# Tables of the rotary angles held behind the last row tile of h instead of the first one

## The chip, the cores and the metric

The kernel runs on one core of a Trainium2 chip. The metric is the device time in microseconds (us) of one execution. Engines are named as in the profile: PE is TensorE's matmul, PEld its weight load, DVE is VectorE, ACT is ScalarE, POOL is GpSimd, SP is SyncE, whose queue issues most transfers. Each engine works through its own instructions in order; waits between engines go by semaphores.

## The reference, cut to what matters

One decoder layer: `h = layer_norm(x) * (1 + scale1) + shift1` with modulation vectors from `silu(c) @ w_ada`, then one input projection of h, from which a causal convolution branch (c_val, c_gate) and a retention branch (q, k, v, g) go on, then an output projection and a gated MLP. What the change touches is the rotation of q and k:

```python
half = x.shape[-1] // 2
inv_freq = ROPE_BASE ** (-jnp.arange(half, dtype=jnp.float32) / half)
ang = positions.astype(jnp.float32)[..., None] * inv_freq
cos = jnp.cos(ang)[:, :, None, :]
sin = jnp.sin(ang)[:, :, None, :]
x1, x2 = x[..., :half], x[..., half:]
return jnp.concatenate([x1 * cos - x2 * sin, x2 * cos + x1 * sin], axis=-1)
```

There are 512 tokens, D_MODEL = 1024, 8 heads of width 128 for q and k.

## The kernel before, in words

All matrix products run as three fp32r products of high and low halves, so a weight and an activation are each split by a copy (the high half, on ACT) and a subtraction (the low half, on DVE).

The first stage, lines 463 to 488, runs over k = 0 to 7, the eight row tiles of h (128 channels by 512 tokens each). In each round `mod_pair` takes two dot products of 1024 on DVE (L378) for the scale and the shift of tile k, PE transposes the normalised x into `xT` (L453), ACT makes `hf` from it (L454) and its high half (L456), DVE the low half (L457), and PE multiplies with six units of weights `w0h`, `w0l` (L480, L481, L484), 18 matmuls of 512 columns. The six sums `u0` to `u5` stay in six of the eight PSUM banks: c_val, c_gate, q, k and two of g for head 0. The other two banks take the transposes.

Behind that stage come the values of heads 0 and 1 (`values`, L554 to L556): 96 matmuls into four banks `v`, with four pieces of weights (`wh`, `wl` 0 to 3 here, made at L146 and L147; three buffers of each). Two of the banks `v` are those of the transposes. The other two come free when ACT has read c_gate (`th`, L515, a tanh) and c_val (`cv`, L517), the first steps of `conv`. `rotary` then reads q and k with the tables `ctab` and `stab` (L534, L535).

`rotary_tables` (L408 to L438) makes these two tables from the positions: the angle in two halves `A1`, `A2`, then five rounds that reduce it modulo a turn, each a pair on ACT that rounds into `tr` (L419, L420) and a step on DVE that takes the fraction `fr` (L424), which is added into `sm` (L428). One more rounding of `fr` stands in the fifth round (L427). Then, for each table, one rounding of `sm`, L433, L434 and four Sin on ACT (L438). `tr`, `fr` and `sm` have one buffer each, so that a round waits for the one before.

The order of instructions on an engine is set when the kernel is built, by a scheduler that takes what is ready by priority. `later(150)` gives the tables a priority 150 steps back, so that they fill gaps. `tc.issue_after(done.ins)` holds all of them until the instruction named has been placed: `done` is the last low half of h (L457) of the round. The 30 taps of a convolution (L525) have the lowest priority (`later(500)`) and fill DVE up through the heads.

Of the kernel before, what the change touches and what calls it, by code (L numbers as in the profile page):

```python
# [20 lines left out]
ND = D // P  # L21
# [157 lines left out]
def block_kernel(ctx: ExitStack, tc: tile.TileContext, a, out):  # L179
# [7 lines left out]
    @contextmanager  # L187
    def later(n):
        p = tc.cur_priority
        tc.cur_priority = p + n  # L190
        yield
        tc.cur_priority = p
# [23 lines left out]
    def vc(name, j=0, w=1):  # L216
        o, _ = VEC[name]
        return vec[:, o + j:o + j + w]
# [38 lines left out]
    def split_to(h, l, src, scale=None):  # L257
        act(h, src, AF.Copy)
        tt(l, src, h.bitcast(F32), ALU.subtract)
# [64 lines left out]
    def ft(tag, shape, dt=F32, bufs=1):  # L324
        uid[0] += 1
        return fp.tile(list(shape), dt, tag=tag, bufs=bufs, name=f"{tag}_{uid[0]}")
# [28 lines left out]
    def load_first(k):  # L355
        wa = ft("wa", [P, 2048], bufs=3)
        w = ft("w0", [P, 768], bufs=3)
        if k == 1:
            nc.sync.dma_start(w, a["w0"][k])
            nc.sync.dma_start(wa, a["wada"][k])  # L360
        else:
            nc.sync.dma_start(wa[:, :D], a["wada"][k][:, :D])
            nc.sync.dma_start(wa[:, D:], a["wada"][k][:, D:])
            nc.sync.dma_start(w, a["w0"][k])
        return wa, w
# [24 lines left out]
    def norm_x(s):  # L390
        rs, nb = layer_stats(xh[s])
        for j in range(2):
            act(xh[s][j], xh[s][j], AF.Identity, bias=nb, scale=rs)
# [14 lines left out]
    def rotary_tables():  # L408
        nc.vector.tensor_copy(A, posi)
        ts(A, A, cc("freq"), None, ALU.mult)  # L410
        nc.vector.tensor_copy(A1r, A)
        tt(A2, A, A1, ALU.subtract)
        c1, c2, c3, c4, c5 = C2PI
        ts(sm, A1, c5, None, ALU.mult)
        for src, c in ((A2, c4), (A1, c4), (A2, c3)):
            stt(sm, src, c, sm, ALU.mult, ALU.add)

        def rnd(dst, src, c=1.0):
            act(dst, src, AF.Identity, bias=cc("magic"), scale=c)  # L419
            act(dst, dst, AF.Identity, bias=cc("magic", 1))  # L420

        for src, c in ((A2, c2), (A1, c3), (A2, c1), (A1, c2), (A1, c1)):
            rnd(tr, src, c)
            stt(fr, src, c, tr, ALU.mult, ALU.subtract)  # L424
            if src is A1 and c == c1:
                rnd(tr, fr)
                tt(fr, fr, tr, ALU.subtract)  # L427
            tt(sm, sm, fr, ALU.add)  # L428
        for tab, shift in ((stab, 0.0), (ctab, 0.25)):
            if shift:  # L430
                ts(sm, sm, shift, None, ALU.add)
            rnd(tr, sm)
            tt(sm, sm, tr, ALU.subtract)  # L433
            ts(fr, sm, 0.49999994, -0.49999994, ALU.min, ALU.max)  # L434
            for half in range(2):
                for dst in range(2):
                    sgn = -1.0 if (dst == 0 and not shift) else 1.0
                    act(tab[64 * dst:64 * dst + 64, half * NT:(half + 1) * NT],  # L438
                        fr[64 * half:64 * half + 64], AF.Sin, scale=sgn * TWO_PI)

    def mod_pair(j, src):
        for t in range(2):
            dot(mods[:, 2 * j + t:2 * j + t + 1], src[:, t * D:(t + 1) * D])
        tt(mods[:, 2 * j:2 * j + 2], mods[:, 2 * j:2 * j + 2], bada[:, 2 * j:2 * j + 2], ALU.add)
# [4 lines left out]
    def first_h(k, hf, c):  # L449

        pt = ps("xT")
        for s in range(c.start // P, c.stop // P):
            nc.tensor.transpose(pt[:, s * P:(s + 1) * P], xh[s][k // 4][:, (k % 4) * P:(k % 4 + 1) * P], ident)  # L453
        act(hf[:, c], pt[:, c], AF.Identity, bias=mods[:, 2 * k + 1:2 * k + 2], scale=mods[:, 2 * k:2 * k + 1])  # L454
        hh, hl = h_h[:, k, c], h_l[:, k, c]
        (act(hh, hf[:, c], AF.Copy) if k else nc.vector.tensor_copy(hh, hf[:, c]))  # L456
        return tt(hl, hf[:, c], hh.bitcast(F32), ALU.subtract)  # L457

    for k in range(ND):
        if k + 2 < ND:  # L460
            lf.append(load_first(k + 2))
        if k == ND - 2:
            st.load(0)
        if k == ND - 1:
            st.load(1)
        wa, w0 = lf[k]
        mod_pair(k, wa)
        hf = ft("hf", [P, S], bufs=2)
        wh = base.tile([P, 768], F32R, tag="wh", bufs=3, name=f"w0h{k}")
        wl = base.tile([P, 768], F32R, tag="wl", bufs=3, name=f"w0l{k}")  # L470
        for n, c in enumerate((slice(0, 256), slice(256, 512)) if k == 0 else (slice(0, 512),)):
            if n:
                norm_x(2)
                norm_x(3)
            done = first_h(k, hf, c)
            if not n:
                split_to(wh, wl, w0)
            for u in range(6):
                w = slice(u * P, (u + 1) * P)
                mm(acc0[u][:, c], wh[:, w], h_h[:, k, c], start=(k == 0 and n == 0), stop=False, skip_group_check=True)  # L480
                mm(acc0[u][:, c], wh[:, w], h_l[:, k, c], start=False, stop=False, skip_group_check=True)  # L481
            for u in range(6):
                w = slice(u * P, (u + 1) * P)
                mm(acc0[u][:, c], wl[:, w], h_h[:, k, c], start=False, stop=(k == ND - 1), skip_group_check=True)  # L484
        if k == 0:
            with later(150), tc.issue_after(done.ins):
                rotary_tables()
            nc.gpsimd.tensor_scalar(bhalf, vc("bin", E_CV, 32), 0.5, None, ALU.mult)
# [39 lines left out]
    def rotary(i, pq, e, nm):  # L528
        sw = ht("sw", [P, S])
        b = vc("bin", e)  # L530
        act(sw[0:64], pq[64:128], AF.Identity, bias=b[64:128])
        act(sw[64:128], pq[0:64], AF.Identity, bias=b[0:64])
        f = ht("t1", [P, S], bufs=2)
        stt(f, pq, b, ctab, ALU.add, ALU.mult)  # L534
        tt(sw, sw, stab, ALU.mult)  # L535
        tt(f, f, sw, ALU.add)
        xh_ = ht(nm + "h", [P, S], F32R, bufs=2 if nm == "q" else 1)
        xl_ = ht(nm + "l", [P, S], F32R, bufs=2 if nm == "q" else 1)
        split_to(xh_, xl_, f)
        return f, xh_, xl_  # L540
# [150 lines left out]
    for i in range(NH):  # L691
        if i == 0:
# [3 lines left out]
            k = rotary(i, pk, E_K + i, "k")  # L696
            v2 = values(i)
        else:
# [14 lines left out]
            k = rotary(i, pk, E_K + i, "k")  # L713
# [149 lines left out]
    for j in range(ND):  # L863
        p_ = ps("yb")
        for half in range(2):
            wh, wl = st.get()
            for kk in range(8):
                k = 8 * half + kk
# [320 lines left out]
    for n, R in enumerate((R1, R2, R2, R2, R1, R3)):  # L1189
# [3 lines left out]
        for q in range(6):  # L1193
# [16 lines left out]
            for kk in range(2 if q < 5 else 1):  # L1210
                k = 2 * q + kk
# [147 lines left out]
```

## Time and profile before

| | |
|---|---|
| median of 3 runs | 1053.08 us (1052.61 to 1053.3) |
| the profiled execution | 1051.99 us |
| its span in the trace | 1050.2 us |
| PE busy | 1025.7 us (98%) |
| DVE busy | 837.3 us (80%) |
| ACT busy | 494.5 us (47%) |

The span is the part of the execution that the trace covers; 1.8 us lie around it. Times in rows are us from the start of the span. A row of the order of time has the start, the busy time, the engine, the line, the operation, output and inputs, and in brackets the idle time of the engine before it with what ended that. In the table of stretches each engine has its busy time and its number of instructions.

### The profile page before, as it was taken

The numbers are of one execution on the slowest core, as the hardware profiler recorded it, in microseconds if no ns is written. First come the engines' busy times: TensorE is split into PE (matmuls) and PEld (weight loads), VectorE is DVE, ScalarE is ACT, GpSimd is POOL, SyncE is SP. The second block draws the span as 40 slices with busy tenths as digits, with TensorE's granted clock in tenths as the row PEclk, the third lists the DMA queues.
The fourth block names the chain that finished last, engine by engine and source line by source line (L and its number), as shares of the span: only waits on it lengthen the run. The fifth ranks groups of instructions, "written<-read, shape, count | busy, mean of one in ns | idle before, by whom it ended". The sixth has DMA issues, their size and how long they took to land.

```text
span 1050.2 us, 12939 instructions
## 1 busy us (share of the span) xinstructions
PE 1025.7 (98%) x4889; PEld 858.6 (82%) x4889; DVE 837.3 (80%) x1373; ACT 494.5 (47%) x766; POOL 72.2 (7%) x93
## 2 busy tenths in 40 slices
PE   5999999999999999999999999999999999999996
PEld 4778888888888888888888888899888888888785
DVE  7979999999789979789994445876666666669888
ACT  5675444443454354461353334264444444457661
POOL 1000302020211020000000000110000000000012
PEclk9999999999999999999999999999999999999998
DMA  9733745482749286368653246012223223245772
GB/s 343 280 107 137 193 146 124 165 190 88 190 154 198 93 252 153 120 227 296 235 224 120 81 165 255 21 41 89 113 81 108 94 87 115 81 155 186 252 218 91
DMA packets 57009, 164.50 MB, mean 157 GB/s; under 512 B 4337, under 2 KB 27121, under 8 KB 47218
## 3 DMA queue, kind: packets, MB, share of 16 engines
q1 hardware_dynamic: 43328, 139.11, 37.9%
q0 software_dynamic: 13328, 24.38, 10.9%
q8 instruction: 38, 0.62, 0.2%
q10 hardware_dynamic: 290, 0.18, 0.1%
q14 instruction: 25, 0.20, 0.1%
HBM read 161.56 MB, written 25.17 MB: 178 GB/s over the span
## 4 chain that ended last, share of the span: by engine, by line
PE 89%; DVE 4%; ACT 3%; DMA 2%; issue 1%; POOL 0%; SPq 0%; DVEq 0%; ACTq 0%; POOLq 0%
PE up L506 7%; PE up L507 7%; PE up L509 7%; PE yb L870 3%; PE gate L506 3%; PE gate L507 3%; PE yb L871 3%; PE yb L872 3%; PE gate L509 3%; PE v L554 3%; PE v L556 3%; PE v L555 3%; PE g L507 2%; PE g L506 2%; PE g L509 2%; PE o L644 2%
## 5 line engine op out<-in xcount | busy, mean ns | idle before, releaser
L147 DVE TENSOR_TENSOR wl<-stage,wh 128x1024 fp32r<-128x1024 f32 x177 | 212.5, 1202 | 100.9 <-PE up L509 57.4
L146 ACT ACTIVATE wh<-stage 128x1024 fp32r<-128x1024 f32 x177 | 184.7, 1044 | 219.5 <-PE up L507 56.1
L525 DVE SCALAR_TENSOR_TENSOR conv<-ci,vec,conv 128x512 f32<-128x512 f32 x240 | 176.8, 747 | 3.4
L506 PE MATMUL up<-h,wh 128*128 128x512 f32 x304 | 118.3, 389 | 0.0
L507 PE MATMUL up<-h,wh 128*128 128x512 f32 x304 | 118.3, 389 | 0.0
L509 PE MATMUL up<-h,wl 128*128 128x512 f32 x304 | 75.1, 389 | 0.0
L509 PEld LDWEIGHTS up<-h,wl 128*128 128x128 f32 x304 | 57.1, 188 | 11.9
L506 PEld LDWEIGHTS up<-h,wh 128*128 128x128 f32 x304 | 57.1, 188 | 11.8
L507 PEld LDWEIGHTS up<-h,wh 128*128 128x128 f32 x304 | 57.1, 188 | 11.8
L1169 PE MATMUL d<-wh,op 128*128 128x512 f32 x132 | 51.4, 391 | 0.7 <-DVE dtmp L1226 0.6
L1170 PE MATMUL d<-wh,op 128*128 128x512 f32 x132 | 51.4, 389 | 0.0
L1171 PE MATMUL d<-wl,op 128*128 128x512 f32 x132 | 51.2, 389 | 0.0
L554 PE MATMUL v<-wh,h 128*128 128x512 f32 x128 | 49.9, 390 | 0.9 <-ACT th L515 0.9
L870 PE MATMUL yb<-rh,wh 128*128 128x512 f32 x128 | 50.3, 393 | 0.0
L506 PE MATMUL gate<-h,wh 128*128 128x512 f32 x128 | 50.1, 392 | 0.0
L872 PE MATMUL yb<-rh,wl 128*128 128x512 f32 x128 | 49.9, 389 | 0.0
L507 PE MATMUL gate<-h,wh 128*128 128x512 f32 x128 | 49.8, 389 | 0.0
L555 PE MATMUL v<-wh,h 128*128 128x512 f32 x128 | 49.8, 389 | 0.0
L871 PE MATMUL yb<-rl,wh 128*128 128x512 f32 x128 | 49.8, 389 | 0.0
L556 PE MATMUL v<-wl,h 128*128 128x512 f32 x128 | 49.8, 389 | 0.0
L1060 ACT ACTIVATE u<-up,vec 128x512 f32<-128x512 f32 x44 | 34.3, 779 | 25.1 <-PE up L509 21.7
L507 PE MATMUL g<-h,wh 128*128 128x512 f32 x112 | 43.7, 390 | 0.0
(317 smaller groups left out, 2398.9 us busy)
## 6 DMA issues: line engine op xcount, KB each, us to landing
stage<-in_wup SPq DMA_DIRECT2D x22, 1024.0 KB, 4.8
stage<-in_wstep SPq DMA_DIRECT2D x21, 1024.0 KB, 4.8
wb<-in_wada SPq DMA_DIRECT2D x32, 512.0 KB, 5.6
stage<-in_wstep SPq DMA_DIRECT2D x16, 512.0 KB, 9.4
stage<-in_wret SPq DMA_DIRECT2D x8, 1024.0 KB, 5.2
stage<-in_wga SPq DMA_DIRECT2D x8, 1024.0 KB, 4.8
wa<-in_wada SPq DMA_DIRECT2D x14, 512.0 KB, 7.1
stage<-T SPq DMA_DIRECT2D x6, 1024.0 KB, 4.8
```

Source lines behind the costliest of these rows:

```text
L146: nc.scalar.activation(wh[:, :w], src, AF.Copy)
L147: nc.vector.tensor_tensor(wl[:, :w], src, wh[:, :w].bitcast(F32), ALU.subtract)
L506: mm(dst, wh[:, k * P:(k + 1) * P], hs[k][0], start=(k == 0), stop=False)
L507: mm(dst, wh[:, k * P:(k + 1) * P], hs[k][1], start=False, stop=False)
L509: mm(dst, wl[:, k * P:(k + 1) * P], hs[k][0], start=False, stop=(k == n - 1))
L525: stt(o, ci[:, t:t + S], vc("cw", i * CK + t), o, ALU.mult, ALU.add)
L554: mm(pv[s], h_h[:, k, sl], wh[:, r], start=(k == 0), stop=False)
L555: mm(pv[s], h_l[:, k, sl], wh[:, r], start=False, stop=False)
L556: mm(pv[s], h_h[:, k, sl], wl[:, r], start=False, stop=(k == ND - 1))
L870: mm(p_, wh[:, w], rs_[k][0], start=(k == 0), stop=False)
L871: mm(p_, wh[:, w], rs_[k][1], start=False, stop=False)
L872: mm(p_, wl[:, w], rs_[k][0], start=False, stop=(k == 15))
```

## The change

`rotary_tables()` with its hold and the small `bhalf` step after it is called in the last round of the row tiles (k = 7) and no longer in the first (k = 0). `done` is then the low half of the last row tile. The instructions are the same.

```diff
@@ -482,7 +482,7 @@
             for u in range(6):
                 w = slice(u * P, (u + 1) * P)
                 mm(acc0[u][:, c], wl[:, w], h_h[:, k, c], start=False, stop=(k == ND - 1), skip_group_check=True)
-        if k == 0:
+        if k == ND - 1:
             with later(150), tc.issue_after(done.ins):
                 rotary_tables()
             nc.gpsimd.tensor_scalar(bhalf, vc("bin", E_CV, 32), 0.5, None, ALU.mult)
```

On DVE at the end of the row tiles, before; `h_163` is the low half of h, `w0l` and `wl` are low halves of weights, `tr`, `fr`, `sm` and `A` belong to the tables:

```order
L444 TENSOR_TENSOR mods<-mods,bada 128x2
L457 TENSOR_TENSOR h_163<-hf_521,h_162 128x512
L424 SCALAR_TENSOR_TENSOR fr_161<-A_23_157,tr_160 128x256
L259 TENSOR_TENSOR w0l_562<-w_68_473,w0h_561 128x768
L457 TENSOR_TENSOR h_163<-hf_560,h_162 128x512
L427 TENSOR_TENSOR fr_161<-fr_161,tr_160 128x256
L428 TENSOR_TENSOR sm_159<-sm_159,fr_161 128x256
L147 TENSOR_TENSOR wl_663<-stage_513,wh_662 128x1024
L147 TENSOR_TENSOR wl_667<-stage_513,wh_666 128x1024
L433 TENSOR_TENSOR sm_159<-sm_159,tr_160 128x256
```

The same place with the change:

```order
L444 TENSOR_TENSOR mods<-mods,bada 128x2
L457 TENSOR_TENSOR h_163<-hf_472,h_162 128x512
L457 TENSOR_TENSOR h_163<-hf_511,h_162 128x512
L409 CAST A_156<-pos_118 128x256
L259 TENSOR_TENSOR w0l_513<-w_68_424,w0h_512 128x768
L410 TENSOR_SCALAR A_156<-A_156,cst 128x256
L411 CAST A_23_157<-A_156 128x256
L147 TENSOR_TENSOR wl_663<-stage_464,wh_662 128x1024
L412 TENSOR_TENSOR A_24_158<-A_156,A_23_157 128x256
L147 TENSOR_TENSOR wl_667<-stage_464,wh_666 128x1024
L414 TENSOR_SCALAR sm_159<-A_23_157 128x256
L424 SCALAR_TENSOR_TENSOR fr_161<-A_24_158,tr_160 128x256
```

Before, the tables are in their fifth round here; with the change their first step stands here.

On ACT at the seventh and eighth row tile (k = 6 and 7), before:

```order
L454 ACTIVATE hf_521<-xT_524,mods 128x512
L419 ACTIVATE tr_160<-A_23_157,cst 128x256
L456 ACTIVATE h_162<-hf_521 128x512
L420 ACTIVATE tr_160<-tr_160,cst 128x256
L454 ACTIVATE hf_560<-xT_563,mods 128x512
```

With the change:

```order
L454 ACTIVATE hf_472<-xT_475,mods 128x512
L454 ACTIVATE hf_511<-xT_514,mods 128x512
L456 ACTIVATE h_162<-hf_472 128x512
L456 ACTIVATE h_162<-hf_511 128x512
L258 ACTIVATE w0h_512<-w_68_424 128x768
```

Between `hf` and the high half of tile 6 stood a step of the tables; now `hf` of tile 7 stands there. Further on, before, `th` (L515) stands behind all eight Sin; with the change behind the first five of them. The weight pieces `wh_662` and `wh_666` stand ahead of the first rounding of the tables with the change, and `wh_670` behind the second round.

On PE where the values first need a bank that `th` frees (`v_660` is the third bank), before, the 19th to the 24th matmul of the values:

```order
L554 MATMUL v_659<-wh_666,h_162 128x512
L555 MATMUL v_659<-wh_666,h_163 128x512
L556 MATMUL v_659<-wl_667,h_162 128x512
L554 MATMUL v_660<-wh_662,h_162 128x512
L555 MATMUL v_660<-wh_662,h_163 128x512
L556 MATMUL v_660<-wl_663,h_162 128x512
```

With the change, the 34th to the 39th:

```order
L554 MATMUL v_659<-wh_670,h_162 128x512
L555 MATMUL v_659<-wh_670,h_163 128x512
L556 MATMUL v_659<-wl_671,h_162 128x512
L554 MATMUL v_660<-wh_662,h_162 128x512
L555 MATMUL v_660<-wh_662,h_163 128x512
L556 MATMUL v_660<-wl_663,h_162 128x512
```

Before, 21 matmuls of the values stand ahead of `v_660`, with the change 36. The remaining 75 and 60 follow it. SP and POOL have the same instructions in the same order.

## Rows read from the trace of the kernel before

**Rows 1.** The page's first part: busy time, share and count by engine.

```profile
PE 1025.7 (98%) x4889; PEld 858.6 (82%) x4889; DVE 837.3 (80%) x1373; ACT 494.5 (47%) x766; POOL 72.2 (7%) x93
```

**Rows 2.** Stretches: length, then PE, PEld, DVE, ACT, POOL, clock, DMA, GB/s.

```profile
30.00:35.00 5.00, 4.55 (x25) 3.53 (x24) 5.00 (x14) 3.17 (x5) 0.00 (x0) 1.00 0.99 374
...
45.00:50.00 5.00, 3.65 (x20) 2.91 (x19) 4.59 (x11) 3.13 (x7) 0.00 (x0) 1.00 0.50 170
...
55.00:60.00 5.00, 5.00 (x23) 4.13 (x22) 2.68 (x6) 3.63 (x7) 0.00 (x0) 1.00 0.70 231
60.00:65.00 5.00, 4.07 (x18) 3.05 (x17) 1.31 (x3) 4.22 (x8) 0.00 (x0) 1.00 0.35 113
```

**Rows 3.** Longest wait of PE from 60 us to the end: total, times, longest.

```profile
PE v L554 <- ACT th L515: 0.9, 1, 0.9
```

**Rows 4.** Order of time, seventh row tile, ACT, DVE and PE.

```profile
47.22 0.78 ACT L454 ACTIVATE hf<-xT,mods 128x512 f32<-128x512 f32 x1 [1.87 <-PE xT L453]
47.90 0.49 ACT L419 ACTIVATE tr<-A,cst 128x256 f32<-128x256 f32 x1
...
48.29 0.62 ACT L456 ACTIVATE h<-hf 128x512 fp32r<-128x512 f32 x1
...
48.94 0.69 DVE L457 TENSOR_TENSOR h<-hf,h 128x512 fp32r<-128x512 f32 x1 [0.37 <-ACT h L456]
...
48.96 1.21 PE L480 MATMUL u<-h,w0h 128*128 128x512 f32 x4 [1.35 <-ACT h L456]
```

**Rows 5.** Order of time, first and 21st matmul of the values, then `th`.

```profile
57.30 0.39 PE L554 MATMUL v<-wh,h 128*128 128x512 f32 x1
...
61.83 0.39 PE L556 MATMUL v<-wl,h 128*128 128x512 f32 x1
62.41 0.69 ACT L515 ACTIVATE th<-u,bhalf 128x512 f32<-128x512 f32 x1
...
63.15 0.50 PE L554 MATMUL v<-wh,h 128*128 128x512 f32 x1 [0.93 <-ACT th L515]
```

**Rows 6.** Order of time, one step of the tables of each kind.

```profile
25.69 0.42 DVE L412 TENSOR_TENSOR A<-A,A 128x256 f32<-128x256 f32 x1
...
43.84 0.42 DVE L424 SCALAR_TENSOR_TENSOR fr<-A,tr 128x256 f32<-128x256 f32 x1
...
44.29 0.51 ACT L419 ACTIVATE tr<-A,cst 128x256 f32<-128x256 f32 x1 [1.58 <-DVE fr L424]
...
44.84 0.51 ACT L420 ACTIVATE tr<-tr,cst 128x256 f32<-128x256 f32 x1
...
57.10 1.68 ACT L438 ACTIVATE stab<-fr 64x256 f32<-64x256 f32 x4
...
60.35 0.29 DVE L434 TENSOR_SCALAR fr<-sm 128x256 f32<-128x256 f32 x1
```

**Rows 7.** The page's groups: splitting a piece of weights; busy, mean ns, idle before.

```profile
L147 DVE TENSOR_TENSOR wl<-stage,wh 128x1024 fp32r<-128x1024 f32 x177 | 212.5, 1202 | 100.9 <-PE up L509 57.4
L146 ACT ACTIVATE wh<-stage 128x1024 fp32r<-128x1024 f32 x177 | 184.7, 1044 | 219.5 <-PE up L507 56.1
```

**Rows 8.** All instructions of line 337 with ns min/median/max: the loads of ACT's tables.

```profile
L337 ACT ACT_TABLE_LOAD  x1: 1283/1283/1283, 2.1 to 2.1; - x1
```

**Rows 9.** Order of time, six matmuls of 256 columns each, PE early on.

```profile
14.46 1.65 PE L480 MATMUL u<-h,w0h 128*128 128x256 f32 x6 [2.38 <-DVE h L456]
...
17.19 1.48 PE L484 MATMUL u<-h,w0l 128*128 128x256 f32 x6
...
23.09 0.88 PE L484 MATMUL u<-h,w0l 128*128 128x256 f32 x6
```

**Rows 10.** Stretches at the span's end, columns as in rows 2.

```profile
1040.00:1045.00 5.00, 0.27 (x3) 0.07 (x1) 4.90 (x11) 0.00 (x0) 1.35 (x2) 0.82 0.28 105
1045.00:1050.00 5.00, 0.00 (x0) 0.00 (x0) 2.20 (x4) 0.00 (x0) 0.62 (x1) 0.50 0.28 105
```

**Rows 11.** A stretch of DVE alone: length, busy time, count, clock, DMA, GB/s.

```profile
280.00:300.00 20.00, 11.57 (x17) 1.00 0.82 295
```

## The prediction

> **What bounds the kernel now.** I read the share of busy time first. PE is busy for 1025.7 of 1050.2 us [rows 1], so time can be lost or won only where PE stands still, and whatever makes PE wait in the middle of the span comes out at its end. Then I looked for those places. Behind 60 us the longest wait of PE is one of 0.9 us, for `th` [rows 3]. Ahead of it, in the stage of the row tiles, PE lacks 0.45 us in the stretch from 30 to 35 us and 1.35 us in that from 45 to 50 [rows 2]. DVE is full there (5.00 of 5), which invites the thought that DVE bounds this stage and that 17 steps of the tables taken away from it would shorten it.
>
> The order of time says otherwise. At the seventh row tile `hf` waits for PE's own transposes, not for DVE, and PE waits for ACT's `h` [rows 4]. PE takes the transposes of this tile only behind the matmuls of the tile before it, and then must wait for `hf` and `h`. That comes from PE's own order, which the change leaves as it is. DVE is full, but ahead of need.
>
> The second view that matters is where `th` is. PE starts the values at 57.30 with two free banks, its 21st matmul starts at 61.83, and `th` runs only at 62.41, behind the last Sin of the tables on ACT. PE goes on at 63.15 [rows 5]. So already before the change, the tables end too late by about a microsecond, and they end that late with 17 of their 24 DVE steps and most of their roundings done below 50 us.
>
> **The change part by part.** *What it removes.* 17 DVE steps of 0.29 to 0.42 us [rows 6] leave the stage of the row tiles, 5 x 0.29 + 12 x 0.42 = 6.5 us of DVE, and ten steps of roundings of about 0.5 us leave ACT. Since PE waits for neither, I price this at nothing. What remains late is PE's own transposes.
>
> *What it does to the seventh tile.* Between `hf` and `h` of tile 6 stood a step of 0.49 us on ACT. With the change `hf` of tile 7 stands there, 0.78 us [rows 4]. `h` starts 0.29 us later, and PE too: the values start at 57.30 + 0.29 = 57.59. Bounds: 0.5 us of gain if nothing stood there, 0.3 us of loss as the order has it; I take the loss.
>
> *When the tables now end.* All 24 DVE steps and 24 ACT steps come behind the low half of tile 7, in one chain, since `tr`, `fr` and `sm` have one buffer each. Two rules for adding up are read off the rows: a step that uses the last one's result starts 0.03 us behind it (43.84 + 0.42 against 44.29), and one that doesn't starts up to 0.1 us before its end (47.22 + 0.78 against 47.90) [rows 4, 6].
> - Start. `hf` 7 ends at 48.68, `h` 6 at 49.20, `h` 7 at 49.72. DVE's low halves of tiles 6 and 7, 0.69 us each [rows 4], end at 49.92 and 50.53. The tables start at 50.45; before, the same point found them in the fifth round.
> - Preparation. On DVE `A` (0.29), the low weights of tile 7 (an estimate from 768 of 1024 columns at 1.20 us: 0.9), two more steps of 0.29, `wl` 0 (1.20) and `A2` (0.42) [rows 6, 7] make 3.4 us, less the overlaps: to 53.7.
> - First round. A rounding is two ACT steps, 0.51 + 0.03 + 0.51 = 1.05 us: to 54.8. DVE meanwhile has `wl` 1 and a step of 0.29, to 55.1. `fr` (0.42) ends at 55.5.
> - Second round. DVE has four steps that depend on each other ahead of `fr`, 4 x 0.45 = 1.8 us, longer than the rounding: `fr` ends at 57.65.
> - Third to fifth. Each 1.05 + 0.42 + 2 x 0.03 = 1.5 us, with 0.45 more in the third, where `wl` 2 stands ahead of `fr`: to 62.6.
> - The extra rounding of `fr`, L427 and L428: 1.08 + 0.42 + 0.45, to 64.55. The rounding of `sm` with L433 and L434: 1.08 + 0.45 + 0.32, to 66.4. Four Sin, 1.68: to 68.1. The second rounding, L433, L434: to 69.95. One Sin, 0.42: to 70.4. `th`, 0.69 + 0.05: PE can go on at 71.15.
>
> *What covers it.* The matmuls of the values follow each other by (61.83 - 57.30) / 20 = 0.2265 us [rows 5]. With the change 36 of them stand ahead of `v_660`: 36 x 0.2265 = 8.15 us, to 57.59 + 8.15 = 65.74. PE then stands still until 71.15, for 5.4 us, where it stood still for 63.15 - (57.30 + 21 x 0.2265) = 1.1 us. Loss: 0.29 + 5.41 - 1.09 = 4.6 us. Bounds on the chain: if none of the other work of ACT and DVE held it up, it would be about 2.2 us shorter (0.9 and 1.2 in the preparation, 0.5 at `wl` 2, less the overlaps) and the loss 2.4 us. If each of its hand-overs took 0.1 us more, with some 20 of them, the loss would be 6.6.
>
> *The clock.* Early on, six matmuls of 256 columns took 1.65 and 1.48 us; at 23.09 the same took 0.88 [rows 9]. PE ran at the lower of its two levels (1.2 GHz against 2.4) from 14.46 until at least 17.19 + 1.48 = 18.67, 4.2 us with hardly a pause, before it rose. At the other end, PE's last matmul ends at 1040.27 and the mean clock from 1040 to 1045 is 0.82, then 0.50 [rows 10]: full for 3.2 us of those five, so it fell 2.9 us after PE had stopped. A rest of 5.4 us is longer than that. So I expect the values to go on at half speed for a while. The start of the program gives at most half of 4.2 = 2.1 us, the other bound is nothing; I take 1.6, nearer to the one row that shows a restart, and less since it was a start from rest of all engines.
>
> *What stands behind the tables.* On ACT `cv`, three Sin, the first tap, `sw`, `sg` and then `wh` 3 queue behind `th`, on DVE `ci`, the taps, L534 and `wl` 3. PE has 36 matmuls on `wh` 0 to 2 behind `th`, to 71.15 + 8.15 = 79.3. Nine ACT steps of 0.4 to 0.7 us, then 1.04 for `wh` 3 and 1.20 for `wl` 3 [rows 7] bring these to about 77.3 and 79.0. That fits, by little. SP's next load into a stage buffer waits for `wl` 3, and is also late, but PE needs it only two units of weights further on.
>
> *Sin and tanh.* With the change `th` stands among the Sin. ACT loaded its tables once, for 1283 ns, at 2.1 us, and never again, though Silu, Sin and tanh follow [rows 8]; so I price the mixing at nothing. The Trainium skill (ScalarE: Activation LUTs, Table sets: the hidden batching unit) says the contrary for functions of different sets: each switch costs a load, so all calls of one set should stand together. If that held here, the two switches behind `th` would add two loads of 1.28 us by the row, 2.6 us on `wh` 3, of which some 2 would reach PE. This case's trace has no second load, so the rule does not bear on these functions.
>
> **The rivals.** (1) *The clock holds* through the rest: the loss is 4.6 us, 1053.08 + 4.6 = 1057.7. For it: the fall at the end came after PE had stopped for good. (2) *DVE's backlog reaches PE.* `ci` starts 8.6 us later than before but PE runs only 4.6 us later, so DVE carries 4 us of taps more through the heads. It first has room from 280 to 300 us, 20 - 11.57 = 8.4 us [rows 11]. If the backlog passes the lead of the weight pieces, up to 4 us come on top of a part of the clock's loss: about 1062. Against it: the taps can be put off, and in the new order fewer of them stand ahead of `wl` 6. (3) *DVE does bound the first stage*, against my reading. Then the 6.5 us of steps taken away bring the values forward by up to 6.5, the tables' start with them, and the total is 4.6 - 6.5 = -1.9, or 1051.2. It decides from 4.6 us of gain on. Against it: rows 4, and PE lacks only 1.8 us in the two stretches named, which can't give 6.5. (4) *The chain is shorter* by the 2.2 us of its lower bound; the rest is then 3.2 us and the clock hardly matters: 1055.5. That the change doesn't do what it says can be excluded: the first step of the tables stands behind the last low half.
>
> **How the numbers follow.** The sum is 1051.99 + 4.6 + 1.6 = 1058.2 for the profiled execution, 1050.2 of span and 1.8 around it. The median of the runs is 1.09 above it, so I add the loss to the median: 1053.08 + 6.2 = 1059.3. Chances: forecast 0.58, clock holds 0.22, backlog 0.08, first stage bound by DVE 0.05, shorter chain 0.07. A measurement of this kernel can tell about 0.2% or 2.1 us. Of the cases only (3) is near or under 1053.08; it is split, 0.03 faster by over 0.2% and 0.02 within, and the weak half of (4) gives 0.03 more within 0.2%: same 0.05, slower 0.92. The range of 1056.0 to 1061.5 holds the forecast with both bounds of the clock, the case where it holds, and halves of (2) and (4).
>
> **What the changed profile would show.** The transposes and matmuls of the row tiles stand where they stood, with PE's start on tile 6 later by 0.3 us, while DVE has gaps below 50 us. The chain of waits runs through `tr`, `fr`, `sm` and Sin between 65 and 71 us. PE has one wait of about 5.4 us for `th`. Behind it matmuls of 512 columns are twice as far apart (0.45 us) for some 3 us, and the granted clock shows a dip. From 90 us on each row stands 6 us later than before. I'm wrong if the values start several microseconds before 57.3 us, if PE's wait for `th` is under 3 us, or if the delay grows or shrinks further on.

## The result, and the profile after

The changed kernel took 1059.09 us, median of 4 runs (1059.01 to 1060.17), the kernel before in the same session 1052.84 (1050.41 to 1053.3). The ratio is 1.0066, with a 95% interval of 1.0054 to 1.0078: slower, as forecast, and 0.2 us from the 1059.3 that was named. The profiled execution took 1059.13 us with a span of 1057.3, so 7.1 us more than that of before (1051.99 and 1050.2). That pair of traces is 0.9 us further apart than the medians; why stands below.

The first part of the page after; [rows 1] answers to it. The columns are busy time, share and count.

```profile
PE 1028.4 (97%) x4889; PEld 860.9 (81%) x4889; DVE 838.1 (79%) x1373; ACT 496.7 (47%) x766; POOL 71.8 (7%) x93
```

The counts are those of before. PE's busy time grew by 2.7 us for the same 4889 matmuls, which already says that some of them ran slower. The rest of the 7.1 us must be time in which PE stood still. The longest waits of PE behind 20 us (total, times, longest) say where; [rows 3] answers to the first line:

```profile
PE v L554 <- ACT th L515: 5.5, 1, 5.5
PE u L480 <- ACT h L456: 1.6, 1, 1.6
```

Next, the order of time on PE, from the last matmul that had a free bank (the 36th of the values) over the rest and on; [rows 5] answers to it.

```profile
64.85 0.39 PE L556 MATMUL v<-wl,h 128*128 128x512 f32 x1
70.72 0.79 PE L554 MATMUL v<-wh,h 128*128 128x512 f32 x1 [5.49 <-ACT th L515]
71.31 0.63 PE L555 MATMUL v<-wh,h 128*128 128x512 f32 x1
71.74 0.63 PE L556 MATMUL v<-wl,h 128*128 128x512 f32 x1
...
76.01 0.63 PE L554 MATMUL v<-wh,h 128*128 128x512 f32 x1
76.44 0.51 PE L555 MATMUL v<-wh,h 128*128 128x512 f32 x1
76.78 0.40 PE L556 MATMUL v<-wl,h 128*128 128x512 f32 x1
77.02 0.39 PE L554 MATMUL v<-wh,h 128*128 128x512 f32 x1
77.24 0.40 PE L555 MATMUL v<-wh,h 128*128 128x512 f32 x1
```

Two things are to be seen. PE stands still for 5.5 us in front of one matmul. And behind it, from 70.72 to 76.5, matmuls of 512 columns start 0.43 us apart, and then 0.23: six microseconds at the lower level of the clock. The table of stretches shows the same (length; PE, PEld, DVE, ACT, POOL; clock; DMA; GB/s):

```profile
65.00:70.00 5.00, 0.23 (x2) 0.00 (x0) 1.73 (x5) 3.27 (x8) 0.00 (x0) 0.98 0.00 0
70.00:75.00 5.00, 4.28 (x10) 3.41 (x11) 2.25 (x4) 4.86 (x10) 0.00 (x0) 0.50 0.00 0
75.00:80.00 5.00, 5.00 (x20) 4.01 (x20) 5.00 (x8) 4.45 (x7) 0.00 (x0) 0.83 0.09 16
```

The granted clock is still 0.98 as the mean of the stretch in which PE rests, and 0.50 in the next. So it fell from 2.4 to 1.2 GHz at about 69.8 (0.2 of the five us at half), 4.6 us after PE's last matmul had ended at 65.24 and 0.9 us before PE went on, and it rose at about 76.7 (0.83: 1.7 us at half).

What PE waited for is one strand of single steps. From the chain of waits (start, us, what), its end:

```profile
64.23 0.52 ACT tr L419
...
64.77 0.52 ACT tr L420
...
65.31 0.44 DVE sm L433
...
65.77 0.30 DVE fr L434
...
66.10 0.34 ACT stab L438
...
67.81 0.52 ACT tr L419
...
68.36 0.52 ACT tr L420
...
68.90 0.44 DVE sm L433
...
69.36 0.30 DVE fr L434
...
70.00 0.68 ACT th L515
...
70.72 0.79 PE v L554
```

`th` waits for none of these. It reads only a sum `u` that had been complete for 13 us. It stands behind the first Sin of `ctab` in ACT's order, and that Sin waits for the strand.

### The profile page after: what moved, and what is told of

Read it like the earlier page. It is cut to its first block, busy times and chain, and to the rows that moved or that the text cites. A ratio compares the mean times of both kernels' runs of the same rounds, so it can differ in the third digit from the quotient of the medians.

```text
span 1057.3 us, 12939 instructions
## 1 busy us (share of the span) xinstructions
PE 1028.4 (97%) x4889; PEld 860.9 (81%) x4889; DVE 838.1 (79%) x1373; ACT 496.7 (47%) x766; POOL 71.8 (7%) x93
## 4 chain that ended last, share of the span: by engine, by line
PE 87%; DVE 6%; ACT 3%; DMA 2%; issue 1%; POOL 0%; SPq 0%; DVEq 0%; ACTq 0%; POOLq 0%
PE up L507 7%; PE up L509 7%; PE up L506 7%; PE yb L870 3%; PE gate L506 3%; PE yb L871 3%; PE gate L507 3%; PE yb L872 3%; PE gate L509 3%; PE v L554 3%; PE v L555 3%; PE v L556 3%; PE g L507 2%; PE g L506 2%; PE g L509 2%; PE o L644 2%
## 5 line engine op out<-in xcount | busy, mean ns | idle before, releaser
L147 DVE TENSOR_TENSOR wl<-stage,wh 128x1024 fp32r<-128x1024 f32 x177 | 212.5, 1202 | 99.4 <-PE up L509 57.5
L146 ACT ACTIVATE wh<-stage 128x1024 fp32r<-128x1024 f32 x177 | 184.9, 1044 | 219.8 <-PE up L507 55.9
L525 DVE SCALAR_TENSOR_TENSOR conv<-ci,vec,conv 128x512 f32<-128x512 f32 x240 | 176.1, 746 | 4.6 <-ACT conv L523 1.4
L506 PE MATMUL up<-h,wh 128*128 128x512 f32 x304 | 118.3, 389 | 0.0
L506 PEld LDWEIGHTS up<-h,wh 128*128 128x128 f32 x304 | 57.1, 188 | 11.8
L554 PE MATMUL v<-wh,h 128*128 128x512 f32 x128 | 51.2, 400 | 5.5 <-ACT th L515 5.5
L555 PE MATMUL v<-wh,h 128*128 128x512 f32 x128 | 50.9, 398 | 0.0
L506 PE MATMUL gate<-h,wh 128*128 128x512 f32 x128 | 50.1, 391 | 0.0
```

The source lines that it names most:

```text
L146: nc.scalar.activation(wh[:, :w], src, AF.Copy)
L147: nc.vector.tensor_tensor(wl[:, :w], src, wh[:, :w].bitcast(F32), ALU.subtract)
L506: mm(dst, wh[:, k * P:(k + 1) * P], hs[k][0], start=(k == 0), stop=False)
L525: stt(o, ci[:, t:t + S], vc("cw", i * CK + t), o, ALU.mult, ALU.add)
L554: mm(pv[s], h_h[:, k, sl], wh[:, r], start=(k == 0), stop=False)
L555: mm(pv[s], h_l[:, k, sl], wh[:, r], start=False, stop=False)
```

## The experiments

One measure serves for all of them: the time from the first matmul of the values (in fill18 and fill12, of the added ones) to the first of the next unit, `cv<-h,wh` (L506 in before). Between the two stand 96 matmuls, and 96 x 0.2266 = 21.75 us is what they take at full clock with no wait. It does not contain the start-up of the program, which differs from run to run by over a microsecond (below). Each number is the difference of two starts in the order of time of that kernel's trace, so it is that of one execution. The median beside it is over all runs: the traced execution of fill12 took 1057.75 us, 2.3 under the median of its runs; those of the others lie within 1.1 us of theirs.

| kernel | values start | `cv` unit starts | between | over 21.75 | median us of the runs |
|---|---|---|---|---|---|
| before | 57.30 | 80.28 | 22.98 | 1.23 | 1052.8 to 1052.9 |
| after | 56.91 | 87.23 | 30.32 | 8.57 | 1059.09 |
| fill18 | 58.33 | 85.88 | 27.55 | 5.80 | 1057.11 |
| fill12 | 57.22 | 86.35 | 29.13 | 7.38 | 1060.08 |
| sin_late | 56.96 | 78.72 | 21.76 | 0.01 | 1050.39 |
| no_tables | 58.23 | 79.98 | 21.75 | 0.00 | 1051.94 |
| hold4 | 58.69 | 82.86 | 24.17 | 2.42 | 1054.34 |
| tr4 | 58.73 | 87.20 | 28.47 | 6.72 | 1059.72 |
| th_first | 57.48 | 84.34 | 26.86 | 5.11 | 1059.41 |

In th_first the rest is the last thing in this stretch, so what the clock cost behind it (1.6 us, see the last section) is not in its number.

My theory: the strand of the tables sets when `th` runs, PE rests for it, and the rest costs PE its clock on top. The rivals: the slow matmuls have another cause than the rest; DVE's load in the first stage is what counts; the strand is long only because of its single buffer.

**Is it the rest that slows the matmuls?** fill18 and fill12 put 18 or 12 more matmuls ahead of the values. Their sums are overwritten by the first true one; nothing of the computation is left out. They fill a part of the rest and delay nothing that `th` needs.

```diff
--- after.py
+++ fill18.py
@@
             wh, wl = st.get()
+            if i == 0 and u == 0:
+                for _ in range(18):
+                    mm(pv[0], h_h[:, 0, 0:P], wh[:, 0:512], start=True, stop=True)
```

> The changed kernel with 18 more matmuls on PE right ahead of the values, into the bank whose first real matmul overwrites them; the result is not touched. They move PE's rest, and do not shorten the chain of the tables. Theory (rest for th plus a fallen clock): PE rests 5.65 - 18 x 0.2266 = 1.6 us in place of 5.65, th still runs at 70.0, the granted clock stays at 1.00, the first matmul behind the values starts at 70.7 + 60 x 0.2266 = 84.3 in place of 87.2, and the time is 1059.1 - 2.9 = 1056.2 us, with more work than the changed kernel. Rival (DVE's backlog makes the loss): it is the same as in the changed kernel, so the time stays at 1059 or above. Rival (PE is the bound here): 18 matmuls more cost 4.1 us, 1063.

fill18 took 1057.11 us (1056.77 to 1058.1, ratio to before 1.0045, 1.003 to 1.006), 2.0 less than after, though it does 18 x 0.2266 = 4.1 us more of work. It is 0.9 us more than was expected; in its trace the values start 1.4 us later than in after (58.33 against 56.91). Its wait row on PE and the stretch behind it:

```profile
72.15 0.50 PE L557 MATMUL v<-wh,h 128*128 128x512 f32 x1 [1.41 <-ACT th L515]
```

```profile
70.00:75.00 5.00, 3.59 (x16) 2.64 (x15) 1.57 (x4) 4.08 (x9) 0.00 (x0) 1.00 0.00 0
```

The rest fell from 5.49 to 1.41, by the 4.1 us of the filling, so `th` did not move with it: PE goes on 13.82 us after the start of the stretch here (72.15 - 58.33) and 13.81 in after (70.72 - 56.91). PE's own work does not decide when `th` runs. The clock stayed at 1.00, and the matmuls behind the rest took 85.88 - 72.15 = 13.73 us, where after has 87.23 - 70.72 = 16.51 for the same 60. So 2.8 us of the loss are the clock's, and they go when the rest shrinks to 1.41 us. In these two traces that leaves no cause for the slow matmuls but the rest.

> As the one with 18, but with 12 more matmuls: the rest should be 5.65 - 12 x 0.2266 = 2.9 us. If the clock holds through a rest of that length, the time is the same as with 18, 1056.2 us, since th sets when PE goes on. If it falls, up to 2.9 us come back, 1057 to 1059. Rival (DVE's backlog): 1059.

fill12, with 12 in the place of 18, took 1060.08 us (1057.75 to 1061.04, ratio 1.0068, 1.0051 to 1.0085): no better than after, and 1.1 us above 1059, the most that was expected if the clock fell. By the total alone it can't be told from the rival of DVE's backlog, which had 1059; its trace decides. That trace is of the shortest of its four executions, 1057.75; the others took 1059.5, 1060.66 and 1061.04, with granted clocks (the mean of the whole execution) of 0.996, 0.994 and 0.992 against its 0.996, and where they lost more stands in no trace. Wait row and stretch:

```profile
71.03 0.56 PE L557 MATMUL v<-wh,h 128*128 128x512 f32 x1 [2.77 <-ACT th L515]
```

```profile
70.00:75.00 5.00, 3.97 (x10) 3.16 (x11) 1.94 (x3) 4.89 (x9) 0.00 (x0) 0.66 0.00 0
```

With a rest of 2.77 us the clock fell, to 0.66 as the mean of this stretch; the 60 matmuls took 86.35 - 71.03 = 15.32, 1.7 us more than 60 x 0.2266 = 13.6. It did not fall in the rest: the mean is still 1.00 from 70 to 71 us and 0.66 from 71 to 72, so the level fell at about 71.3, 0.3 us after PE had gone on and 3.1 us after the end of its last matmul at 68.26. A rest of 1.41 us left the clock at full and this one did not; hold4 (below) has one of 2.11.

**Is it the strand in front of `th`?** sin_late goes the other way. The rounds of the tables stay behind the first row tile as before; `th` and `cv` are written in the last row tile, and only the last part of the tables (the roundings of `sm`, L433, L434 and the Sin) is held behind them.

```diff
--- before.py
+++ sin_late.py
@@
             tt(sm, sm, fr, ALU.add)
+    def rotary_sins():
         for tab, shift in ((stab, 0.0), (ctab, 0.25)):
@@
             nc.gpsimd.tensor_scalar(bhalf, vc("bin", E_CV, 32), 0.5, None, ALU.mult)
+        if k == ND - 1:
+            read = conv(0, acc0[0], acc0[1])
+            with later(150), tc.issue_after(read.ins):
+                rotary_sins()
...
         if i == 0:
             pcv, pcg, pq, pk, pg0, pg1 = acc0
-            conv(i, pcv, pcg)
```

> The kernel before, with the five rounds of the tables left where they were, but the last part (rounding of sm, L433, L434, the eight Sin) held behind th and cv of head 0. Theory (what th waits for is the end of the tables): PE's wait of 0.93 us for th is gone, all values run without a rest, and the time is 1.1 us under that of the kernel before, 1051.8 us. Rival (the tables are needed so early that a later Sin makes q and k late): PE waits for a bank of q, k or g, or for rotated k at the heads, and the time is 1053 or above.

It took 1050.39 us, median of 10 runs (1049.32 to 1051.89), against 1052.82 for before in 19 runs: ratio 0.9981 (0.9969 to 0.9992). That is faster than both kernels, by 0.8 to 3.3 us against before, and 1.4 us under what was expected. On ACT:

```profile
56.77 0.67 ACT L464 ACTIVATE th<-u,bhalf 128x512 f32<-128x512 f32 x1
57.34 0.68 ACT L466 ACTIVATE cv<-u,bhalf 128x512 f32<-128x512 f32 x1
59.81 1.68 ACT L439 ACTIVATE stab<-fr 64x256 f32<-64x256 f32 x4
63.92 1.70 ACT L439 ACTIVATE ctab<-fr 64x256 f32<-64x256 f32 x4 [0.40 <-DVE fr L435]
```

`th` runs 0.2 us ahead of the first matmul of the values. PE has no wait at all in them, and the 96 matmuls take 21.76. The Sin end at 65.6 and hold up nobody. Before lost 1.23 us here, the wait of [rows 3] and the uneven pace around it; sin_late has that back. The medians differ by 2.4 us; that the rest of it is more than the scatter of the runs is not shown. Among the runs whose granted clock, the mean of the whole execution, is 0.997 or more, the medians are 1050.22 (6 runs) and 1051.37 (10 runs of before), 1.15 apart.

**Does DVE bound the first stage?** no_tables leaves the tables out and fills them with 1 and 0, so q and k are not rotated. The 24 steps of DVE and the 24 of ACT (16 roundings, 8 Sin) are gone.

```diff
--- before.py
+++ no_tables.py
@@
             with later(150), tc.issue_after(done.ins):
-                rotary_tables()
+                nc.vector.memset(stab, 0.0)
+                nc.vector.memset(ctab, 1.0)
```

> The kernel before with the tables left out: ctab is set to 1 and stab to 0, so q and k are not rotated and the output differs. Theory (PE's own order bounds the stage of the row tiles): the values start at 57.3 give or take 0.6, PE has no wait for th, and the time is 0.8 to 1.1 us under that of the kernel before, 1051.8 to 1052.1 us. Rival (DVE bounds that stage, where it is full): with 6.5 us of DVE steps gone the values start at about 51, and the time is about 1046 us.

It took 1051.94 us (10 runs, 1050.63 to 1052.74; ratio 0.9992, 0.9982 to 1.0001). If DVE bound the first stage, 6.5 us of its steps would have come off; nothing that can be told from before did. The stretches at start-up and at the seventh row tile:

```profile
20.00:25.00 5.00, 4.67 (x24) 4.47 (x25) 4.89 (x12) 2.52 (x4) 0.00 (x0) 0.66 1.03 406
...
45.00:50.00 5.00, 3.38 (x20) 2.70 (x18) 2.18 (x6) 2.10 (x4) 0.00 (x0) 1.00 0.74 250
```

From 45 to 50 us DVE is down to 2.18 us of work (4.59 in [rows 2]), and PE lacks as much there as before, 1.6 us against 1.35. That rival falls. The first line is another matter: the mean clock of 0.66 says that it was low for 3.4 of these five us; before and after both have 1.00 there. The values start at 58.23 here, 1.3 us later than the 56.9 of after and sin_late, though less work stands ahead of them.

**How does the loss grow with the round?** hold4 moves the tables half as far, behind the row tile k = 4.

```diff
--- before.py
+++ hold4.py
@@
-        if k == 0:
+        if k == 4:
             with later(150), tc.issue_after(done.ins):
```

> The kernel before with the tables held behind the low half of the fifth row tile (k = 4) in place of the first. PE again has 36 matmuls of the values ahead of the third bank, as in the changed kernel, but two rounds of the tables stand ahead of the weight piece wh 2 that stood behind it. Theory (th waits for the end of one chain): th runs at about 66.4 us instead of 70.0, PE rests 2.0 us instead of 5.65, the time is 0.9 to 1.2 us above the kernel before if the clock holds, and up to 2.9 us more if it falls: 1054 to 1057. Rival (what counts is that the tables leave the first stage at all, by what DVE then carries later): most of the loss of the changed kernel is there, in step with the 10 of 24 DVE steps moved.

It took 1054.34 us (10 runs, 1053.34 to 1055.76; ratio 1.0018, 1.0008 to 1.0028): slower than before by a fifth of a per cent. Wait row and stretch:

```profile
69.12 0.50 PE L554 MATMUL v<-wh,h 128*128 128x512 f32 x1 [2.11 <-ACT th L515]
```

```profile
65.00:70.00 5.00, 2.89 (x13) 2.07 (x12) 1.05 (x3) 4.07 (x9) 0.00 (x0) 1.00 0.00 0
```

The rest is 2.11 us and the clock stays at 1.00; the 60 matmuls take 82.86 - 69.12 = 13.74. So the loss is not proportional to the move. Half the way costs 2.42 - 1.23 = 1.2 us in the values, the whole way 7.3: at half the way a longer rest alone, at the whole way the clock too. That a rest of 2.11 us is always free is not shown; this is one trace.

**Is the single buffer what makes the strand long?** tr4 gives `tr` four buffers, so that roundings may run ahead of the fractions.

```diff
--- after.py
+++ tr4.py
@@
-    tr = ft("tr", [P, NT])
+    trs = [ft(f"tr{n}", [P, NT]) for n in range(4)]
+    tr = trs[0]
@@
-        for src, c in ((A2, c2), (A1, c3), (A2, c1), (A1, c2), (A1, c1)):
+        for n, (src, c) in enumerate(((A2, c2), (A1, c3), (A2, c1), (A1, c2), (A1, c1))):
+            tr = trs[n % 4]
```

> The changed kernel with four buffers for the rounded product in place of one, so that the roundings of a round do not wait for the fraction of the round before. Same instructions. Theory (the chain of the tables, not its amount of work, sets th): four roundings move ahead of wh 2 and th runs 1.2 us earlier, at about 68.8 us; PE's rest goes from 5.65 to about 4.5 us. The clock still falls, so the time is 1.2 us under the changed kernel, give or take 1.5 for the clock. Rival (ACT's or DVE's amount of work sets th): th stays at 70.0.

It took 1059.72 us (6 runs, two of them near 1057 and four near 1060, 1056.53 to 1060.52; ratio 1.0055, 1.0037 to 1.0074), which can't be told from after; 1.2 us less was expected. The trace can: its wait row is

```profile
71.29 0.80 PE L556 MATMUL v<-wh,h 128*128 128x512 f32 x1 [4.24 <-ACT th L517]
```

The rest is 1.25 us shorter than in after. The strand from its first step (51.62 here, 49.79 in after) to `th` (70.57, 70.00) is 18.95 against 20.21 us. Only the first rounds got shorter. From the extra rounding of `fr` on (62.73 here, 62.17 in after) to `th` the two strands take 7.84 and 7.83 us. The profiled run had the low clock at start-up, so that its values start at 58.73, which hid the gain in the total of that run. The buffer is a small part of it: rounding, fraction, sum and Sin depend on each other.

**Would it do to put `th` ahead of the tables?** th_first keeps the tables behind the last row tile, but behind `th` and `cv` too, with all their roundings and Sin.

```diff
--- after.py
+++ th_first.py
@@
+        if k == 0:
+            nc.gpsimd.tensor_scalar(bhalf, vc("bin", E_CV, 32), 0.5, None, ALU.mult)
         if k == ND - 1:
-            with later(150), tc.issue_after(done.ins):
+            read = conv(0, acc0[0], acc0[1])
+            with later(150), tc.issue_after(read.ins):
                 rotary_tables()
-            nc.gpsimd.tensor_scalar(bhalf, vc("bin", E_CV, 32), 0.5, None, ALU.mult)
...
-            conv(i, pcv, pcg)
```

> The changed kernel with th, cv and the first steps of head 0's convolution ahead of all roundings and Sin of the tables on ACT. Theory in its narrow form (only th in front of the values matters): PE has no rest at the values, as in the kernel with the Sin held behind th, and the time is about 1050 to 1052 us. Theory in its wider form (whatever holds a bank that PE needs next): with the roundings behind th and the taps of the convolution between them, the tables end at about 84 us; q, k and g of head 0 are read only then, PE finds no free bank when the values end at 79 to 80 us, and rests some 6 us there, with a fallen clock behind: 1056 to 1061.

It took 1059.41 us (4 runs, 1059.07 to 1059.93; ratio 1.0064, 1.0044 to 1.0084), as slow as after, where the theory that only `th` stands wrong had it at 1052 at most. `th` runs at 57.28 and the values have no wait. The rest stands one unit further on. From the order of time, ACT first, then PE:

```profile
81.35 0.84 ACT L438 ACTIVATE ctab<-fr 64x256 f32<-64x256 f32 x2
82.20 0.68 ACT L535 ACTIVATE sw<-u,vec 64x512 f32<-64x512 f32 x1
82.90 0.68 ACT L536 ACTIVATE sw<-u,vec 64x512 f32<-64x512 f32 x1
83.60 1.26 ACT L582 ACTIVATE sg<-u,vec 128x512 f32<-128x512 f32 x2
```

```profile
84.34 0.80 PE L525 MATMUL cv<-h,wh 128*128 128x512 f32 x1 [4.95 <-ACT sg L582]
84.94 0.63 PE L526 MATMUL cv<-h,wh 128*128 128x512 f32 x1
85.37 0.63 PE L525 MATMUL cv<-h,wh 128*128 128x512 f32 x1
```

The next unit needs a bank that `sg` frees, `sg` stands behind both `sw`, and those behind the last Sin. The Sin even end at 82.2, 9.7 us later than in after (71.27 + 1.27). Of these, 5.4 us are a later start: the first rounding stands behind `th` and `cv`, at 58.42 where after has it at 53.04. The other 4.3 us are a longer strand. The chain of waits of this kernel (start, us, what) shows what stretched the strand:

```profile
71.24 0.34 DVE fr L427
71.58 0.66 DVE conv L473
72.24 0.34 DVE sm L428
72.58 0.68 DVE conv L473
```

The taps of the convolution, set free early by `th` and `cv`, stand between its steps on DVE, and on ACT a split of weights stands ahead of the last two Sin (L146 at 80.27, 1.06 us). The pace of PE behind the rest is the low clock's again. Whoever reads the wait row of after as "`th` stands in the wrong place" is misled: the strand is late for all readers of `u`, and `th` is only the first of them.

In this pair the stage itself is cheaper than in after: `d`, the last product, starts at 939.32 against 940.64. The end gives it back. 0.7 us go at PE (a wait of 0.53 for a low half of weights among them), 0.8 us behind its last matmul, which hold4 and tr4 also show. What decides that tail stays open.

## Why the prediction was right, and where its terms were not

The pair of traces, term by term. The sum of the last column is the 6.95 us by which the `cv` unit starts later (87.23 against 80.28); from there to PE's last matmul both take 960 us.

| term | predicted | measured |
|---|---|---|
| values start | +0.29 | -0.39 |
| longer rest | 5.41 - 1.09 = +4.32 | 5.65 - 1.09 = +4.56 |
| clock | +1.6 (0 to 2.1) | +2.91 |
| uneven pace behind `th` in before | not named | -0.13 |

*The seventh tile.* The term was right and its sum was not. The rows of after, to be read against [rows 4]:

```profile
46.58 1.45 ACT L454 ACTIVATE hf<-xT,mods 128x512 f32<-128x512 f32 x2 [5.95 <-PE xT L453]
47.92 1.15 ACT L456 ACTIVATE h<-hf 128x512 fp32r<-128x512 f32 x2
48.60 1.20 PE L480 MATMUL u<-h,w0h 128*128 128x512 f32 x4 [1.62 <-ACT h L456]
```

The two `hf` stand in one row now, ahead of `h`, and PE's wait grew from 1.35 to 1.62, by 0.27 where 0.29 was forecast. In no_tables, which has this order on ACT and no tables at all, it is 1.6 too. But start-up varies, and it went the other way. The first transposed tile stands ahead of every instruction that the change moves; its row in before, and then in after:

```profile
9.71 0.47 PE L453 MATMUL xT<-cst,x 128*128 128x128 f32 x1 [0.81 <-ACT x L393]
```

```profile
9.16 0.47 PE L453 MATMUL xT<-cst,x 128*128 128x128 f32 x1 [0.26 <-ACT x L393]
```

After began this work 0.55 us earlier, and the transposes of the seventh tile 0.63 us earlier (45.95 against 46.58).

*The strand.* From its first step to `th` it took 20.21 us (49.79 to 70.00); the forecast had 19.95 (50.45 to 70.4). Adding up single steps with the hand-overs read from two rows was right to 0.3 us over some 45 steps, other work of both engines included. No large errors cancel in it: counted from that first step, each joint of the list came within 0.4 us of its forecast.

*The rest.* 5.65 against 5.41: the 36 matmuls ahead of it were counted right, and both errors above come together in it.

*The clock.* This is the mis-sized term: 1.6 was taken and 2.1 given as the upper bound, and 2.91 came. The step that failed is the bound. It took the one restart that the trace of before shows, 4.2 us at the low level, as the longest, though its own "until at least" makes 4.2 a lower limit; after the rest the level stayed low for 6.0 us of work (70.72 to 76.7). That restart was also read from the pace of [rows 9] alone: the stretches of before from 10 to 20 us have a mean granted clock of 1.00, so there the record of the clock does not show what the pace does. The rival that the clock holds falls by the same rows. That it fell at all was judged from the right row (2.9 us after PE's last matmul), though here it took 4.6 us. (Some 0.13 of the 2.91 go with any restart, and did in before: fill18 and hold4, with the clock at full, need 13.73 and 13.74 for the 60 matmuls.)

*DVE in the first stage.* DVE has 2.24 us of work from 45 to 50 us, and PE is no faster for it:

```profile
45.00:50.00 5.00, 3.38 (x19) 2.68 (x18) 2.24 (x7) 3.42 (x6) 0.00 (x0) 1.00 0.09 31
280.00:300.00 20.00, 20.00 (x100) 16.76 (x99) 15.15 (x23) 12.29 (x20) 5.28 (x7) 1.00 0.95 273
```

With no_tables that rival is gone for good. *The backlog:* the second line answers to [rows 11]. DVE has 15.15 us of work where it had 11.57, 3.6 us more, which looks like the 4 us of the forecast. But only 2.2 us of it are taps (L525 has 5.23 us there and 2.99 before). At the same point of PE's work (6.93 us later in after) DVE was behind by 2.3 us of taps at 100 us and by 1.6 at 280, and by 300 it had caught up. The 4 us rest on a `ci` that starts 8.6 us later, which the prediction's rows don't give: its own times for `th` (70.4 and 62.41) make it 8.0. It started 7.6 us later (71.28 against 63.70). PE is busy for all of the 20 us, and the backlog never reached it: the delay is 6.9 us at 472 us, at 567 us and at 940 us alike.

*What stands behind `th`.* `wh` 3 was due at 77.3 and `wl` 3 at 79.0:

```profile
75.96 1.06 ACT L146 ACTIVATE wh<-stage 128x1024 fp32r<-128x1024 f32 x1
```

```profile
77.39 1.22 DVE L147 TENSOR_TENSOR wl<-stage,wh 128x1024 fp32r<-128x1024 f32 x1
```

They end at 77.0 and 78.6, and PE, which was slower than forecast by then, did not wait. *Sin and tanh:* the trace of after has one load of ACT's tables, of 1283 ns at 2.2 us, as in [rows 8]. The rule of the Trainium skill that was weighed (ScalarE: Activation LUTs, Table sets: the hidden batching unit) does not bear on these functions: `th` starts 0.32 us behind the start of a Sin, and behind `cv` the next Sin follows with hardly a gap (71.27, where `cv` ends at 71.24).

*The total.* The three terms make 7.1 us in the pair, and the medians differ by 6.25. The profiled execution of before lay 0.85 us under the median of its four runs; that of after was at its median. So that the total came within 0.2 us of the forecast is luck, and it fits better than its parts: the clock was 1.3 us too small, the start 0.7 us too late, most of that by a start-up that the change doesn't touch, and the median of before took up the rest.

## What to carry to other kernels

A strand of small dependent steps that fills gaps costs nothing as long as it ends before something in order behind it on the same engine is needed: hold it back, and everything that queues behind it, the readers that free PSUM banks above all, is late by as much as the strand ends later (`th` by 7.6 us here, 70.00 against 62.41). Ask of filler work what stands behind it, and put the readers of a finished sum ahead of the part of the filler that must wait (sin_late); to move a reader alone helps little if the next ones stay behind the strand (th_first). A rest of the matmul engine can have a second price in the clock: in one trace each, it was nothing for rests of 1.4 and 2.1 us and 1.6 to 2.9 us for rests of 2.8 to 5.5 us.

## What was not expected of the hardware

The price of a rest does not grow with its length. By the rows of these runs (the rest, and what the work behind it lost to the low level): 1.41 us, none; 2.11, none; 2.77, 1.7 us; 4.24, 2.3 us (87.20 - 71.29 less 13.6); 4.95, 1.6 us (16 matmuls from 84.34 to 89.30, less 15 x 0.2266); 5.49, 2.9 us. Each price is about half of the time that PE then worked at the low level (3.4, 4.6, 3.1 and 6.0 us in these four), and that time did not follow the rest. Nor did the fall come at a fixed time: by the mean clock of single microseconds it came 2.1 us after the end of PE's last matmul in tr4 (69.1), 3.1 in fill12 (71.3), and 4.6 in after and th_first (69.8, 84.0), so that a rest of 2.11 us, free in hold4, may not be so in another run. The Trainium skill (TensorE: Matmul & The Clock Gate, Part 1) says that one kernel has more or fewer slow matmuls at its start from run to run. These rows, one trace each of different kernels and behind a rest, fit that and do not show it: the kernel with the rest of 4.95 us paid less than that with 4.24.

The clock differs from trace to trace at the start of the program too. In four of nine traces (hold4, tr4, fill18, no_tables) the mean clock from 20 to 25 us is 0.66 and the values start at 58.2 to 58.7; in the other five, before and after among them, it is 1.00 and they start at 56.9 to 57.5. That this is what spreads the runs of before from 1050.41 to 1055.28 us is likely: of the 35 runs of before in the two sessions of the experiments, the 15 with a granted clock of 0.997 or more as the mean of the execution have a median of 1051.41 us, the other 20 one of 1053.54. It is not all of it, since the run of 1055.28 us had 0.997, and where in a run the clock was low only its trace would show.
